# A two-layer trunk's mixer: the convolution branch joined before the recurrent one, its norm taken into the last scan

## The chip, the cores and the metric

The kernel runs on one core of one Trainium2 chip. The time is that of one execution on the device in microseconds (us). All data are float32; one launch computes the whole function.

## The reference, cut to what matters

Two layers, each a half-step feed-forward, a mixer and a second half-step feed-forward, with a layer norm after each. 16 learned tokens stand ahead of 512, so there are 528 positions of width 1024. The change lies in the mixer's end.

```python
def _conv_branch(glu_a, glu_b, conv_w, conv_b, ln_g, ln_b, wo):
    u = glu_a * jax.nn.sigmoid(glu_b)
    kern = conv_w[:, None, :].astype(u.dtype)
    u = lax.conv_general_dilated(u, kern, window_strides=(1,),
                                 padding=[(CONV_WIDTH - 1, 0)],
                                 dimension_numbers=("NWC", "WIO", "NWC"),
                                 feature_group_count=D_CONV) + conv_b
    u = jax.nn.silu(_layer_norm(u, ln_g, ln_b))
    return u @ wo

def _rwkv_branch(zr, time_mix, w0, w_up, a0, a_up, g_up, k_k, k_a, r_k, lnx_g, lnx_b, wo):
    ...
    y = _rwkv7_scan(rh, decay.reshape(B, L, H, N), kh, vh, kk, ah)
    mu = jnp.mean(y, axis=-1, keepdims=True)
    var = jnp.mean(jnp.square(y - mu), axis=-1, keepdims=True)
    y = ((y - mu) * lax.rsqrt(var + GN_EPS)).reshape(B, L, D_RWKV)
    y = y * lnx_g.astype(jnp.float32) + lnx_b.astype(jnp.float32)
    ...
    y = (y + bonus.reshape(B, L, D_RWKV)).astype(zr.dtype) * g
    return y @ wo

def _mixer(x, w_in, time_mix, conv_w, conv_b, conv_ln_g, conv_ln_b, conv_wo,
           w0, w_up, a0, a_up, g_up, k_k, k_a, r_k, lnx_g, lnx_b, rwkv_wo, w_out):
    z = x @ w_in
    ...
    h = jax.nn.sigmoid(gate_c) * yc + jax.nn.sigmoid(gate_r) * yr
    return h @ w_out
```

## The kernel before, in words

Activations lie channel-major: 128 channels on the partitions, 8 tiles of them, positions along the free axis (528 in layer 0; 512 in layer 1's tail, where the learned tokens are dropped). Each large product is done in three float32r products: a weight and an input are both split into a rounded high part and a rest (`w_hi`, `w_lo`; `xh`, `xl`), and hi*hi, hi*lo and lo*hi are summed. One output tile of 128 channels ("a column") therefore takes 8 x 3 x 2 = 48 products, two halves of 264 (or 256) positions. A weight column comes by a 512 KB load to `w_raw` (two buffers), ScalarE rounds it (`w_hi`), and VectorE subtracts (`w_lo`, L160); for the gate columns the rest is made by an adding DMA on POOL's queue.

In a mixer, after the projections, the recurrence is done in four scans (quarters q = 0 to 3 of the heads), each of 8 steps. A step is a chain: TensorE products (L1416), ScalarE copy `w` (L1418), TensorE (L1429, L1432), ScalarE copy `va` (L1435), TensorE (L1438), VectorE state update `sv` (L1444, L1445), and the next step's L1416. TensorE's waits in this chain are filled by `filler`: the projections of the gates (`gate`, L246 products, result `glus` stored to DRAM). VectorE does the taps of the convolution (`taps`, L1089) in its gaps. After a scan, `post` normalizes the scan's output by heads (`group_norm`), transposes it on TensorE (L1540) and stores it to DRAM (`yscr`).

The order on each engine comes from the Tile framework's scheduler, which takes instructions by priority in program order; `high_priority(offset=...)` shifts a part, and `nosync` fixes one instruction behind another without a semaphore. An engine runs its instructions strictly in that order.

At the end of the fourth scan stand 30 products of a constant block of ones (`keep`, L227), then the transposes of the second half, the last gate projection, 22 more constant products. Then `mixer_end` opens a new set of rooms: the recurrent branch is loaded, split (`rh`, `rl`, L113) and multiplied by `rwkv_wo`, first two columns together. The convolution's output (`cscr`) is loaded there too, summed over tiles (`ssum`, L469), and normed by `layer_norm` (L415 mean, L420 subtract, L422 square, L439 variance, L443 square root, L444 reciprocal, L450 scale, L457 SiLU, L112/L113 split into `bh`, `bl`) while TensorE works on the remaining columns. Then come eight columns with `conv_wo`, eight with `w_out`, and the norm `ln2`.

PSUM rooms: `mm` has two buffers in the mixer and six in `mixer_end`.

## Time and profile before

| | |
|---|---|
| median of 3 runs | 3038.53 us (3034.16 to 3048.38) |
| the profiled execution | 3036.81 us, its span 3035.1 us |
| mean granted TensorE clock | 0.992 |
| VectorE, ScalarE busy | 75%, 47% of the span |
| chain that ended last | TensorE 81%, VectorE 8%, DMA 4%, ScalarE 3% |
| mixer's end, layer 0 | last scan ends near 982 us, `conv_wo` columns end near 1104 us |
| mixer's end, layer 1 | last scan ends near 2487 us |

The page gives busy time by engine, the groups of instructions, and the chain that ended last. With TensorE busy nearly all the time, what a change is worth shows in two places: products that need not be done, and the few gaps of TensorE, each with the instruction that ended it. "Busy" of TensorE adds overlapping products only once, so the pace of products is read from a stretch of time and its count. A window's row gives the stretch's length, then for each engine its busy time and count, the granted clock (1.00 is full speed), and the DMA share.

### The profile page before, as it was taken

How to read it: one execution, taken by the hardware profiler on the slowest of the kernel's cores; microseconds unless marked ns; L12 is line 12 of the kernel's file. 1: busy time of each engine (PE TensorE's matmuls, PEld its weight loads, DVE VectorE, ACT ScalarE, POOL GpSimd, SP SyncE). 2: the span in 40 equal slices, each digit the busy share in tenths (PEclk: the TensorE clock that was granted, in tenths of full speed). 3: DMA queues.
4: the chain of work that ended last, by engine and by line, in shares of the span. 5: the costliest groups of instructions: out<-in, count | busy, mean ns of one | idle time of the engine just before them, and what ended most of it. 6: DMA issues, size and time to landing. Idle time of an engine off the chain costs nothing.

```text
span 3035.1 us, 65020 instructions
## 1 busy us (share of the span) xinstructions
PE 2961.4 (98%) x26524; PEld 2832.8 (93%) x26524; DVE 2282.9 (75%) x4689; ACT 1435.9 (47%) x2553; POOL 181.5 (6%) x288
## 2 busy tenths in 40 slices
PE   9999999999999999999999999999999999999998
PEld 9999989888888999999999999899888889999998
DVE  6666777898876768676776767779988758677767
ACT  4544454344554535444444444543454556255443
POOL 0110000000000000100001000000000010001100
PEclk9999999999999999999999999999999999999999
DMA  7565534335465554565555654443354555456661
GB/s 200 141 146 128 128 128 146 97 97 126 109 152 132 181 157 117 129 153 126 129 130 137 146 133 121 134 143 99 98 136 116 137 148 174 138 134 148 149 147 53
DMA packets 556152, 405.33 MB, mean 134 GB/s; under 512 B 89306, under 2 KB 500798, under 8 KB 555854
## 3 DMA queue, kind: packets, MB, share of 16 engines
q1 hardware_dynamic: 520302, 308.49, 35.6%
q0 software_dynamic: 30944, 84.18, 15.0%
q10 hardware_dynamic: 4608, 8.52, 0.8%
q8 instruction: 208, 3.41, 0.5%
q14 instruction: 90, 0.74, 0.1%
HBM read 270.81 MB, written 47.12 MB: 105 GB/s over the span
## 4 chain that ended last, share of the span: by engine, by line
PE 81%; DVE 8%; DMA 4%; ACT 3%; issue 2%; SPq 1%; ACTq 0%; POOL 0%; POOLq 0%; DVEq 0%
PE mm L217 54%; PE mm L246 15%; PE sc L1341 2%; DVE cacc L1089 1%; PE sc L1260 1%; PE tr L1416 1%; PE ch L1429 1%; PE ch L1438 1%; DMA w_raw<-in_w_in_dram 1%; DMA a<-ascr 1%; DMA w_lo<-w_raw 1%; DVE w_lo L160 1%; PE sc L1012 1%; DVE ln_rstd L444 1%; SPq L1309 1%
## 5 line engine op out<-in xcount | busy, mean ns | idle before, releaser
L217 PE MATMUL mm<-xh,w_hi 128*128 128x264 f32 (+1 forms) x1792 | 510.4, 286 | 6.9 <-ACT xh L460 5.4
L217 PE MATMUL mm<-xl,w_hi 128*128 128x264 f32 (+1 forms) x1792 | 509.2, 285 | 0.7 <-DVE xl L461 0.3
L217 PE MATMUL mm<-xh,w_lo 128*128 128x264 f32 (+1 forms) x1792 | 507.8, 284 | 0.0
L217 PE MATMUL mm<-hh,w_hi 128*128 128x264 f32 (+1 forms) x1408 | 399.9, 284 | 1.3 <-ACT hh L112 1.3
L217 PE MATMUL mm<-hh,w_lo 128*128 128x264 f32 (+1 forms) x1408 | 400.0, 284 | 0.0
L217 PE MATMUL mm<-hl,w_hi 128*128 128x264 f32 (+1 forms) x1408 | 399.6, 284 | 0.2
L246 PE MATMUL mm<-xh,w_lo 128*128 128x264 f32 x1760 | 380.9, 294 | 10.9 <-DMA w_lo<-w_raw 10.6
L246 PE MATMUL mm<-xh,w_hi 128*128 128x264 f32 x1760 | 383.5, 294 | 4.1 <-DVE tmp L962 2.3
L246 PE MATMUL mm<-xl,w_hi 128*128 128x264 f32 x1760 | 380.2, 292 | 0.0
L1089 DVE SCALAR_TENSOR_TENSOR cacc<-cu,cw,cacc 128x528 f32<-128x528 f32 (+1 forms) x480 | 355.5, 752 | 5.1 <-ACT cacc L1087 1.4
L217 PEld LDWEIGHTS mm<-xh,w_hi 128*128 128x128 f32 x1792 | 337.2, 189 | 10.8 <-ACT xh L460 7.9
L217 PEld LDWEIGHTS mm<-xl,w_hi 128*128 128x128 f32 x1792 | 339.1, 189 | 2.7 <-DVE xl L461 2.5
L217 PEld LDWEIGHTS mm<-xh,w_lo 128*128 128x128 f32 x1792 | 338.8, 189 | 0.0
L122 ACT CAST w_hi<-sums 128x512 fp32r<-128x512 f32 (+1 forms) x204 | 154.7, 759 | 314.8 <-PE mm L217 205.4
L246 PEld LDWEIGHTS mm<-xh,w_lo 128*128 128x128 f32 x1760 | 277.4, 190 | 19.5 <-DMA w_lo<-w_raw 12.0
L246 PEld LDWEIGHTS mm<-xh,w_hi 128*128 128x128 f32 x1760 | 278.2, 190 | 14.5 <-DVE tmp L962 2.8
L246 PEld LDWEIGHTS mm<-xl,w_hi 128*128 128x128 f32 x1760 | 277.7, 189 | 5.6
L217 PEld LDWEIGHTS mm<-hh,w_hi 128*128 128x128 f32 x1408 | 264.9, 188 | 1.9 <-ACT hh L112 1.7
L217 PEld LDWEIGHTS mm<-hl,w_hi 128*128 128x128 f32 x1408 | 265.1, 188 | 0.9 <-DVE hl L113 0.8
L217 PEld LDWEIGHTS mm<-hh,w_lo 128*128 128x128 f32 x1408 | 265.5, 189 | 0.1
L160 DVE TENSOR_TENSOR w_lo<-w_raw,w_hi 128x1024 fp32r<-128x1024 f32 (+1 forms) x194 | 204.1, 1054 | 67.3 <-ACT w_hi L149 64.2
L149 ACT CAST w_hi<-w_raw 128x1024 fp32r<-128x1024 f32 x134 | 140.4, 1049 | 232.5 <-PE mm L246 63.6
(367 smaller groups left out, 6752.8 us busy)
## 6 DMA issues: line engine op xcount, KB each, us to landing
w_raw<-in_w_in_dram SPq DMA_DIRECT2D x116, 512.0 KB
w_lo<-w_raw POOLq DMA_DIRECT2D x100, 512.0 KB, 5.0
w_raw<-in_ffn_wg_dram SPq DMA_DIRECT2D x88, 512.0 KB
w_raw<-in_ffn_wu_dram SPq DMA_DIRECT2D x88, 512.0 KB
w_raw<-in_ffn_wd_dram SPq DMA_DIRECT2D x80, 512.0 KB
w_lo<-w_raw POOLq DMA_DIRECT2D x68, 256.0 KB, 3.5
w_raw<-in_rwkv_wo_dram SPq DMA_DIRECT2D x16, 512.0 KB
w_raw<-in_conv_wo_dram SPq DMA_DIRECT2D x16, 512.0 KB
```

Of the source, the lines that this page charges most:

```text
L122: self.nc.scalar.copy(hi, x)
L149: copy = self.nc.scalar.copy(hi[:, :kt], raw[:, :kt])
L160: sub = self.nc.vector.tensor_tensor(lo[:, k], raw[:, k], hi[:, k].bitcast(F32), op=ALU.subtract)
L217: self.issued = self.nc.tensor.matmul(pm, a[:, k, :], b[:, xk + k, s], start=first and k == 0 and j == 0, stop=last and k == nk - 1 and j ...
L246: m = self.issued = nc.tensor.matmul(pm[:, h, :n], a[:, wk + k, :], b[:, xk + k, s:s + n], start=first and k == 0 and j == 0, stop=last an ...
L444: nc.vector.reciprocal(rstd[:, :n], rstd[:, :n])
L1012: nc.tensor.matmul(pm, w[a][r, o, :], x[b][r, s], start=j == 0, stop=j == 2)
L1089: tap = nc.vector.scalar_tensor_tensor(y, x, w, y, op0=ALU.mult, op1=ALU.add)
L1260: pairs.append(nc.tensor.matmul(ps[:, e, p * P:(p + 1) * P], FB[p][r, fs], G[r, p, 1, :, cs], start=True, stop=True))
L1309: nc.sync.dma_start(out=dd[o:o + NM, g * N // 2:(g + 1) * N // 2, f, r], in_=self.xd[q, g, f, k:k + N // 2] .rearrange("s t i -> t s i"))
L1341: nc.tensor.matmul(ps[r, i], vt[r, i], x[r, i], start=True, stop=True)
L1416: nc.tensor.matmul(tr[0:C, right(h)], G[:, h // 2, h % 2, 0, cs], sv[:, h, :], start=True, stop=True)
```

## The change

The convolution branch is finished first. All its taps are done by the start of the fourth scan; its output is summed and averaged there (`conv_mean`) and normed during that scan (`conv_norm`), in rooms that are given back at its first step (pool `early`, on the right side of the memory, followed by pool `late`). Both products with a constant block at this place are gone, with their numbers (`KEEPM`). Behind the scan the eight `conv_wo` columns come first, in the mixer's own PSUM rooms (`conv_out`), the first two together; the recurrent branch is loaded and multiplied in `mixer_end` behind them and added. The gates' order is turned to match, one more gate projection is placed ahead of the fourth scan (`FILLS`), and `post` of the fourth scan uses the same rooms as the others. In `layer_norm` the tiny square root that fetches ScalarE's table is fixed behind the last subtraction, so that it no longer stands far ahead of its use.

```diff
-YR = (0, 3, 6)
+YR = (0, 3, 6, 8)
-FILLS = (3, 3, 4, 2)
+FILLS = (3, 3, 5, 2)
+SUMS_EARLY = 1000
-TAP = ((6, 6, 6, 6, 6, 6, 6, 6), (4, 4, 4, 4, 4, 4, 4, 4), (4, 4, 4, 4, 4, 4, 4, 4), (6, 6, 6, 6, 6, 0, 0, 0))
+TAP = ((6, 6, 6, 6, 6, 6, 6, 6), (4, 4, 4, 4, 4, 4, 4, 4), (4, 4, 4, 4, 4, 4, 4, 4), ())
-KEEPM = (30, 22)
...
+                    if q == 3:
+                        self.tap_late = 150
+                        self.taps(KT * TAPS)
+                        mean = self.conv_mean()
                     self.inverse(q, 1, Q)
...
+                if q == 3 and c == 0:
+                    self.leave(epool)
+                    lpool, self.lp3 = self.enter(f"late{l}", side="right")
+                    hc, yc = self.conv_rooms()
+                elif q < 3:
+                    self.taps(TAP[q][c])
...
+        filler(len(fill))
+        room = self.mp.tile([P, 4, KT, P], F32R, name="sb", bufs=1)
+        early = [self.unit("conv_wo", o, [room[:, 2 * o], room[:, 2 * o + 1]])
+                 for o in range(JHEAD)]
+        self.conv_norm(*mean, hc, yc)
         for _ in post:
             pass
-        filler(len(fill) - LAST)
-        self.later = self.turned
-        filler(len(fill))
-        self.later = None
-        self.keep(self.sc()[:, 0], KEEPM[1])
-        self.taps(KT * TAPS)
         self.cuts = 1
-        self.leave(cpool)
+        self.conv_out(early, hc, yc)
...
+    def conv_mean(self):
+        ...
+        for a, b in zip(CV, CV[1:]):
+            nc.sync.dma_start(out=cv[:, a:b], in_=csv[:, a:b, s])
+        ssum, mean = (mp.tile([P, T], F32, name="v", bufs=4)[:, 0:2 * n] for _ in range(2))
+        for o in range(1, KT):
+            nc.vector.tensor_tensor(ssum, cv[:, 0] if o == 1 else ssum, cv[:, o], op=ALU.add)
+        nc.scalar.copy(mean.rearrange("p (h t) -> p h t", h=2), self.over_partitions(ssum))
+
+    def conv_norm(self, cv, rstd, mean, hc, yc):
+        ...
+        for k in range(0, KT, 2):
+            nc.vector.tensor_tensor(cv[:, k:k + 2], cv[:, k:k + 2],
+                                    mean[:, None].to_broadcast([P, 2, 2 * n]), op=ALU.subtract)
+            nc.scalar.activation(hc[:, k:k + 2, s], cv[:, k:k + 2], AF.Square)
+            if k:
+                nc.vector.tensor_tensor(hc[:, 0:2, s], hc[:, 0:2, s], hc[:, k:k + 2, s],
+                                        op=ALU.add)
+        total = hc[:, 0, s]
+        nc.vector.tensor_tensor(total, total, hc[:, 1, s], op=ALU.add)
+        with self.tc.high_priority(offset=SUMS_EARLY):
+            var = self.over_partitions(total)
+        nc.scalar.activation(rstd.rearrange("p (h t) -> p h t", h=2), var, AF.Sqrt,
+                             bias=self.eps[:, 0:1])
+        nc.vector.reciprocal(rstd, rstd)
+        for o in range(KT):
+            z = cv[:, o]
+            nc.vector.scalar_tensor_tensor(z, z, self.v1("conv_ln_g", o, self.vec), rstd,
+                                           op0=ALU.mult, op1=ALU.mult)
+            nc.scalar.activation(z, z, AF.Silu, bias=self.v1("conv_ln_b", o, self.vec))
+            self.split(z, yc[0][:, o, s], yc[1][:, o, s])
+
+    def conv_out(self, early, h, x):
+        ...
+        self.later = self.scanned
+        for os in [range(JHEAD)] + [(o,) for o in range(JHEAD, KT)]:
+            cols = [(o, early[o] if o < JHEAD else self.unit("conv_wo", o), self.gate_load(o), self.mm()) for o in os]
+            self.together([self.mac1(pm[:, i, :n], w, x, t, KT)
+                           for o, w, g, pm in cols for i, t in enumerate(tok)])
+            for o, w, g, pm in cols:
+                for i, t in enumerate(tok):
+                    self.nc.vector.scalar_tensor_tensor(
+                        h[:, o, t], g[:, t], 1.0, pm[:, i, :n], op0=ALU.add, op1=ALU.mult)
...
             elif p == 0 and g:
                 self.group_norm(ysb[:, 2:4], P, 2)
-                self.issued = self.scanned
-                self.keep(self.sc()[:, 0], KEEPM[0])
...
-            nc.scalar.activation(rstd[:, 0:1], eps, AF.Sqrt)
+            self.nosync(nc.scalar.activation(rstd[:, 0:1], eps, AF.Sqrt), sub)
```

On TensorE at the end of layer 0's fourth scan, before (L1438 is the last step's output product, L227 the constant products, L1540 the transposes of the scan's second half, L246 gate projections):

```order
L1438 MATMUL ch<-va,sb 64x64 x4
L227 MATMUL sc<-ones 128x512 x30
L1540 MATMUL tr<-ident,b_11530 128x128 x2
L1540 MATMUL ch<-ident,b_11530 128x128 x2
L246 MATMUL mm<-xl,w_hi 128x264
L246 MATMUL mm<-xh,w_lo 128x264 x2
```

The same place of the change, around the variance's sum (L933), the last step (L1503, L1516 and so on; L251 are gate projections):

```order
L1525 MATMUL ch<-va,sb 64x64 x8
L251 MATMUL mm<-xl,w_hi 128x264
L933 MATMUL sc<-a,ones 128x264 x2
L251 MATMUL mm<-xh,w_lo 128x264 x2
L251 MATMUL mm<-xh,w_hi 128x264 x2
L1503 MATMUL tr<-sv,G 64x64 x4
```

and its start of the convolution's columns (L1615 and L1618 are the transposes of the scan's first half, L219 the products of `conv_out`):

```order
L251 MATMUL mm<-xh,w_lo 128x264 x2
L1615 MATMUL tr<-ident,small 128x16
L1618 MATMUL tr<-ident,b_11591 128x128 x2
L1615 MATMUL ch<-ident,small 128x16
L1618 MATMUL ch<-ident,b_11591 128x128 x2
L219 MATMUL mm<-bh,sb 128x264 x2
```

What moved: the constant products are gone, the transposes of the second half follow only 24 products into the third `conv_wo` column, and the columns themselves stand where the last gate projection and the recurrent columns stood. In layer 1 one whole gate projection still stands between the scan's end and these columns, behind a first single product of `bh`.

On ScalarE, from the copy ahead of the variance to the first part of the normed tile (L964 is the square root, L1505 and L1522 the copies `w` and `va` of the last step, L1188 a gate's tanh, L154 the rounding of the first two `conv_wo` columns, L971 the SiLU, L122 the copy to `bh`):

```order
L964 ACT_TABLE_LOAD
L964 ACTIVATE v<-sc,eps 128x528
L1505 COPY w_12242<-tr 64x256
L1188 ACT_TABLE_LOAD
L1188 ACTIVATE glus<-mm 128x528
L1522 COPY va<-ch 64x256
L1190 DMA gscr_4672<-glus 128x528
L1538 COPY b_11591<-ch 64x256
L154 CAST sb<-w_raw 128x512 x4
L971 ACT_TABLE_LOAD
L971 ACTIVATE G<-G,vec 128x528
L122 CAST bh<-G 128x528
```

Three table loads now stand within the last step and behind it, where before no load stood.

On VectorE, behind the last part of the normed tile (L123), ahead of the first results of the convolution's columns (L994); L1578, L1580 and L1581 belong to the group norm of the scan's second half, L165 makes the `w_lo` of the third and fourth column:

```order
L123 TENSOR_TENSOR bl<-G,bh 128x528
L1623 TENSOR_TENSOR yf<-yf,gg 128x272
L1578 TENSOR_TENSOR b_11591<-b_11591,gn_st 128x512
L165 TENSOR_TENSOR w_lo<-w_raw,w_hi 128x1024
L1580 TENSOR_REDUCE gn_st<-b_12528 128x8
L165 TENSOR_TENSOR w_lo<-w_raw,w_hi 128x1024
L1581 TENSOR_SCALAR gn_st<-gn_st 128x8
L994 SCALAR_TENSOR_TENSOR a<-ln_sq,mm 128x264
L402 TENSOR_SCALAR rs_12535<-gn_st 128x8
L994 SCALAR_TENSOR_TENSOR a<-ln_sq,mm 128x264
```

Before, the group norm had VectorE to itself while the 30 constant products ran; now both the norm's tail and two weight columns stand ahead of it, and the two L994 that empty the first column's PSUM room come behind them.

More of the change, by code (lines that the diff above doesn't have):

```diff
@@ L138, in wunit @@
             load = self.loading = self.nc.sync.dma_start(out=raw[r, :kt], in_=src)
-            if self.behind is not None:
-                self.nosync(load, self.behind)
-                self.behind = None
         n = kt // self.cuts
@@ L149, in wunit @@
             copy = self.nc.scalar.copy(hi[:, :kt], raw[:, :kt])
-            if self.first is not None:
-                self.nosync(copy, self.first[0])
         if dma:
@@ L220, in mac1 @@
                 self.log.append(self.issued)
+                if self.later is not None:
+                    self.nosync(self.issued, self.later)
+                    self.later = None
             yield
@@ L299, in setup @@
         self.cuts = 1
-        self.behind = None
-        self.first = None
         self.issued = None
         self.log = []
+        self.later = None
     def fetch_x(self, h, room, after=None):
@@ L819, in mixer @@
         self.ring(self.w0)
-        mpool, self.mp = self.enter(f"mix{l}")
+        mpool, rest = self.enter(f"mix{l}")
+        epool, room = self.enter(f"early{l}", side="right")
+        self.mp = self.cvp = Rooms(room, rest)
         self.smask = self.mp.tile([P, T], F32, name="smask")
@@ L905, in mixer, with conv_rooms, over_partitions @@
-        self.taps(KT * TAPS)
         self.cuts = 1
-        self.leave(cpool)
+        self.conv_out(early, hc, yc)
         self.leave(mpool)
         self.leave(ppool)
-        return self.mixer_end(more(l + 1))
+        return self.mixer_end(more(l + 1), hc, lpool)
+    def conv_rooms(self):
+        return (self.lp3.tile([P, KT, T], F32, name="a", bufs=1),
+                [self.lp3.tile([P, KT, T], F32R, name="b" + x, bufs=1) for x in "hl"])
+    def over_partitions(self, x):
+        ps, n = self.sc(), self.n
+        for h in range(2):
+            self.nc.tensor.matmul(ps[:, h, :n], self.ones, x[:, h * n:(h + 1) * n],
+                                  start=True, stop=True)
+        return ps[:, :, :n]
@@ L931, in places @@
             tile(name, (NM, NM), 2)
+        self.cut = [tile(f"cu{i}", (TAPS - 1 + T,)) for i in range(2)]
+        tile("cacc", (T,), 2)
     def mm(self):
@@ L1604, in mixer_end @@
         yrv = self.ys.rearrange("(o p) t -> p o t", p=P)
-        def fetch(a, b):
-            load = nc.gpsimd.dma_start(out=h[:, a:b, s], in_=yrv[:, a:b, s])
+        for a, b in zip(YR, YR[1:]):
+            nc.gpsimd.dma_start(out=r[:, a:b, s], in_=yrv[:, a:b, s])
             for o in range(a, b):
-                self.parted = self.split(h[:, o, s], yr[0][:, o, s], yr[1][:, o, s])
-            return load
-        loads = [fetch(a, b) for a, b in zip(YR, YR[1:])]
-        if BEHIND is not None:
-            self.behind = loads[BEHIND]
@@ L1615, in mixer_end @@
-        early = [unit("rwkv_wo", o) for o in range(JHEAD)]
-        for a, b in zip(CV, CV[1:]):
-            if a == CV[YRLATE]:
-                fetch(KT - 2, KT)
-            nc.sync.dma_start(out=cv[:, a:b, s], in_=csv[:, a:b, s])
-        if YRLATE == len(CV) - 1:
-            fetch(KT - 2, KT)
-        for o in range(KT):
-            add = self.add_sum(ssum, cv, o, s)
-            if o == 1:
-                self.nosync(add, self.parted[1])
-        for i in range(2):
-            for _ in self.layer_norm(i, cv, ssum, t0, n, "conv_ln_g", "conv_ln_b", jp, st, yc,
-                                     self.vec, silu=True):
-                pass
@@ L1637, in mixer_end @@
                 op0=ALU.mult, op1=ALU.add)
-        gated(KT, "conv_wo", yc, h, False)
-        hp = parts("r")
+        for o in range(KT):
+            w, g = self.unit("rwkv_wo", o), self.gate_load(KT + o)
+            for i in tok:
+                po, gv = mm()[:, :n], g[:, i]
+                self.together([self.mac1(po, w, yr, i, KT)])
+                nc.vector.scalar_tensor_tensor(gv, gv, 1.0, po, op0=ALU.add, op1=ALU.mult)
+                nc.vector.tensor_tensor(h[:, o, i], h[:, o, i], gv, op=ALU.add)
+        hp = parts(late, "b")
         for o in range(KT):
```

127 lines of the change are left out of this document (56 added, 71 removed).

## The prediction

> **What bounds the kernel now.** First the page's busy times by engine, then the waits of TensorE by releaser (us of idle time, number, longest), then TensorE's timeline at both mixers' ends (start, us, engine, line, and in brackets the idle time before the row with its releaser).
>
> ```profile
> PE 2961.4 (98%) x26524; PEld 2832.8 (93%) x26524; DVE 2282.9 (75%) x4689; ACT 1435.9 (47%) x2553; POOL 181.5 (6%) x288
> PE mm L246 <- DMA w_lo<-w_raw: 10.6, 7, 2.6
> ...
> PE st L415 <- DVE ssum L469: 11.9, 6, 4.6
> ```
>
> TensorE is 98% busy, so time goes only where its products go or where one of its few gaps closes. The waits for `ssum` lie, the two longest of them, at the two mixers' ends, and so do the constant products:
>
> ```profile
> 981.95 7.10 PE L227 MATMUL sc<-ones 128*128 128x512 f32 x30
> 988.88 0.38 PE L1540 MATMUL tr<-ident,b 128*128 128x128 f32 x2
> ...
> 997.01 5.20 PE L227 MATMUL sc<-ones 128*128 128x512 f32 x22
> 1002.04 0.53 PE L217 MATMUL mm<-rh,w_hi 128*128 128x264 f32 x3
> ...
> 1017.71 0.92 PE L415 MATMUL st<-ssum,ones 128*128 128x264 f32 x2 [4.64 <-DVE ssum L469]
> ...
> 2486.73 7.14 PE L227 MATMUL sc<-ones 128*128 128x512 f32 x30
> 2493.70 0.38 PE L1540 MATMUL tr<-ident,b 128*128 128x128 f32 x2
> ...
> 2502.19 5.17 PE L227 MATMUL sc<-ones 128*128 128x512 f32 x22
> 2507.20 0.52 PE L217 MATMUL mm<-rh,w_hi 128*128 128x256 f32 x3
> ...
> 2521.82 1.22 PE L415 MATMUL st<-ssum,ones 128*128 128x256 f32 x2 [3.91 <-DVE ssum L469]
> ```
>
> The products behind the waits are slow (two take 0.92 and 1.22 us, where three of that width take 0.53 at 1002.04), so the windows there count too: length, then for each engine (TensorE, its weight load, VectorE, ScalarE, GpSimd) busy time and count, then granted clock, DMA share and its GB/s.
>
> ```profile
> 1018.00:1021.00 3.00, 3.00 (x14) 2.87 (x14) 2.79 (x4) 1.69 (x3) 0.00 (x0) 0.51 0.30 97
> 1021.00:1024.00 3.00, 3.00 (x25) 3.00 (x24) 2.47 (x7) 1.77 (x2) 0.00 (x0) 0.92 0.05 9
> 2521.00:2524.00 3.00, 2.18 (x8) 2.00 (x9) 2.41 (x5) 1.04 (x1) 0.00 (x0) 0.50 0.55 152
> 2524.00:2527.00 3.00, 3.00 (x17) 3.00 (x17) 2.58 (x5) 2.86 (x3) 0.00 (x0) 0.54 0.15 55
> 1060.00:1080.00 20.00, 20.00 (x167) 20.00 (x166) 16.57 (x30) 10.34 (x15) 0.00 (x0) 1.00 0.61 172
> ```
>
> After each wait the granted clock is about a half for 3 to 6 us. The last row is a stretch without gaps: 20/167 = 0.12 us a product, 5.8 us for a column of 48.
>
> **What goes.** Between the first constant product and the next row lie 988.88 − 981.95 = 6.93 and 1002.04 − 997.01 = 5.03 us in layer 0, 6.97 and 5.01 in layer 1: **23.9 us**. The two waits are 4.64 + 3.91 = **8.55 us**. Clock: busy time times what is missing to 1.00 is (1 − 0.51)·3.00 + (1 − 0.92)·3.00 = 1.7 and (1 − 0.50)·2.18 + (1 − 0.54)·3.00 = 2.5, **4.2 us**. Together 36.7. Real work only changes places: gate projections, `rwkv_wo` and `conv_wo` columns and the sums over partitions are as many as before.
>
> **What comes instead.** The constant products gave cover. Behind the first block the group norm of the scan's second half ran on VectorE:
>
> ```profile
> 982.45 0.69 DVE L1476 TENSOR_REDUCE gn_st<-b 128x8 f32<-128x512 f32 x1 [3.91 <-ACT b L1451]
> ...
> 987.97 0.69 DVE L1497 TENSOR_TENSOR b<-b,rs 128x512 f32<-128x512 f32 x1
> ```
>
> that is 6.2 us with a dozen tiny steps between. Now its cover must be `conv_wo` products, and these need the convolution's norm, whose variance leaves TensorE only in the last scan step. The prices of the norm's steps (groups by line: busy us, mean ns of one, idle before):
>
> ```profile
> L160 DVE TENSOR_TENSOR w_lo<-w_raw,w_hi 128x1024 fp32r<-128x1024 f32 x15 | 18.3, 1220 | 9.6 <-ACT w_hi L149 9.6
> L147 ACT CAST w_hi<-w_raw 128x512 fp32r<-128x512 f32 x14 | 8.5, 616 | 3.6 <-PE mm L246 3.6
> L1591 DVE SCALAR_TENSOR_TENSOR h<-g,mm 128x264 f32<-128x264 f32 x16 | 6.6, 420 | 1.0 <-PE mm L217 0.8
> L1101 ACT ACTIVATE glus<-mm 128x528 f32<-128x528 f32 x9 | 5.5, 607 | 6.7 <-PE mm L246 6.7
> L113 DVE TENSOR_TENSOR rl<-h,rh 128x528 fp32r<-128x528 f32 x8 | 5.2, 704 | 2.6 <-ACT rh L112 2.5
> L420 DVE TENSOR_TENSOR a<-a,st 128x1056 f32<-128x1056 f32 x4 | 4.9, 1236 | 0.2 <-PE st L415 0.2
> L112 ACT CAST rh<-h 128x528 fp32r<-128x528 f32 x8 | 4.6, 630 | 1.3 <-DMA h<-yscr 1.3
> L444 DVE RECIPROCAL ln_rstd<-ln_rstd 128x264 f32<-128x264 f32 x2 | 3.6, 1800 | 0.1
> L1089 DVE SCALAR_TENSOR_TENSOR cacc<-cu,cw,cacc 128x528 f32<-128x528 f32 (+1 forms) x480 | 355.5, 752 | 5.1 <-ACT cacc L1087 1.4
> ```
>
> The new orders hold table loads, whose row of before is:
>
> ```profile
> 1032.35 1.28 ACT L457 ACT_TABLE_LOAD   x1
> 1033.65 0.92 ACT L457 ACTIVATE a<-a,vec 128x264 f32<-128x264 f32 x2
> ```
>
> I follow the chain by hand from V, the end of the variance's sum (L933), in layer 0.
> - VectorE: load 1.28 and square root (as long as two of 264, some 1.0, and hand-overs) end at V + 2.6; a reciprocal of 528 (two of 1.80) at 6.2; the scaling (0.75, as L1089) at 6.95.
> - ScalarE: copy `w` at 3.0, second load at 4.3, tanh 0.6, copy `va` at 5.3, then four casts for the `conv_wo` columns (0.62 each, free to write only after the last step reads its rooms, about V + 6.3) to 9.2, third load to 10.5, SiLU 0.65, copy 0.6: `bh` at V + 11.8. The difference (0.7, as L113) gives `bl` at 12.5.
> - TensorE: last output product at about V + 5.5, 23 gate products (2.8), transposes and hand-overs: at the columns by about V + 10.4.
> - Then each of the other seven tiles costs VectorE 0.75 + 0.70 = 1.46 (ScalarE 1.25), with some 1.7 of the group norm's pieces among them: last `bl` at V + 24.4, last 12 products (1.43) at 25.9. TensorE alone would be done at 10.4 + 11.5 = 21.9: **4.0 us** of waiting.
> - The third column needs the first one's PSUM room. Ahead of the two L994 that empty it stand L1623, three pieces of the group norm (0.4 + 0.7 + 0.7 + 0.2), two L165 of 1.22 and one more tiny step; with 0.42 for each L994 that is 5.4, so V + 29.8: **3.9 us**.
> - After 24 products the transposes wait for the rest of the group norm, a dozen steps of 0.2 and 0.69: **0.7 us**.
>
> Layer 0: 8.6. In layer 1 the order differs: one `bh` product, then a whole gate projection (5.8 us) that covers the norm. The product waits for `bh` (13.3 against 10.3), **3.0**; then `w_lo` 0.3, second PSUM room 1.0, third column's 0.6, transposes 0.2: 5.1. Sum **13.7 us**. Behind the waiting products stand on TensorE the rest of the first two columns, the group norm's transposes and every later column, so nothing of it is hidden. These are hand estimates; their ends are nothing (the norm done before TensorE comes) and a chain that starts one scan step (5.4 us, D's rows) later in each layer, 13.7 + 10.8 = 24.5. I take the middle because V stands in the last step in both layers' orders.
>
> The clock after new waits goes by the nearest row: a wait of 3.9 like the removed one of 3.91 (2.5 us), a wait of 3.0 like this one (fences: the wait, another of its kind, and two windows):
>
> ```profile
> 916.53 0.30 PE L1334 MATMUL sc<-dd,ut 64*64 64x64 f32 x2 [1.50 <-DMA dd<-xdscr]
> ...
> 2420.89 0.39 PE L1334 MATMUL sc<-dd,ut 64*64 64x64 f32 x2 [2.76 <-DMA dd<-xdscr]
> ```
>
> ```profile
> 2420.00:2425.00 5.00, 4.11 (x39) 3.67 (x40) 0.83 (x2) 0.00 (x0) 0.00 (x0) 0.60 0.20 18
> 2425.00:2430.00 5.00, 5.00 (x48) 4.65 (x48) 2.78 (x4) 0.61 (x1) 0.00 (x0) 0.72 0.73 202
> ```
>
> (1 − 0.60)·4.11 + (1 − 0.72)·5.00 = 3.0. Together **5.5 us**. The Trainium skill, page "TensorE: Matmul & The Clock Gate", section "What's actually happening", sets half rate only after an idle window of about 3.4 us, and full rate after as long of work; by it the 3.0-us wait would be free and the sum some 4 us lower. No run of before bears that out for waits: the clock was 0.60 after 2.76 us, and the row decides.
>
> **Smaller terms.** The convolution's output is now loaded on SP's queue ahead of the fourth scan. Before, that load stood in the chain that ended last (start, us):
>
> ```profile
> 1004.83 5.62 DMA a<-cscr
> ```
>
> The last column's load of this kind, and seven additions of 0.7, are some 11 us, two scan steps; the mean's sum stands in the scan's second step. I take 0; one wait like 2.76 with its clock in each layer, 12, would be the other end. The loads for the recurrent columns move behind the `conv_wo` columns on the same queue, with 46 us of products ahead of them: 0. The two waits for `dd`, above, stand ahead of the third and fourth scans, where the turned gates now put one more projection (5.8 us): I let them go with their clock, 1.5 + 2.8 + 3.0 = −7. Against it, gate projections that follow one another wait for `w_lo` (10.6/7 = 1.5 each by the wait row; I take two, +3), and the fourth scan takes the norm's work between its steps (+2): **−2**, with ends at −7 and at the stretch priced under D. The square root fixed behind the subtraction: its load was hidden beside other work before and stays there, 0, at most one load of 1.28 in each of five norms (+6). Later columns have a 5.8-us product stretch for every weight's 2 × 0.62 and 1.22, so 0.
>
> **Sum.** −36.7 + 13.7 + 5.5 − 2 = −19.5. The profiled execution took 3036.8 us (span 3035.1), 1.7 below the median of the three. 3036.8 − 19.5 = 3017.3; I forecast **3017**.
>
> **Rivals.**
> - **B: the norm's waits are hidden.** If V comes earlier than the last step, or the gate projections reach over it as in layer 1, only the removal counts: 3036.8 − 36.7 = 3000. For: layer 1's order has that cover. Against: in layer 0 the first `conv_wo` product stands directly behind the scan's end.
> - **C: the waits are as long as those removed.** The order puts three loads, a reciprocal, 16 VectorE operations and the group norm behind V; one step's delay in each layer gives back 10.8 and some 4 of clock, so about 3032 (3027 to 3037). This is also the case in which the change does not do what it says, the norm running behind the scan and not in it.
> - **D: slower.** The state update that starts the next step queues on VectorE behind the norm's 128x1056 operations.
>
> ```profile
> 966.35 0.43 DVE L1444 TENSOR_TENSOR sv<-ch,sv 64x256 f32<-64x256 f32 x1
> ...
> 971.72 0.43 DVE L1444 TENSOR_TENSOR sv<-ch,sv 64x256 f32<-64x256 f32 x1
> 960.00:982.00 22.00, 21.80 (x252) 18.78 (x252) 11.94 (x47) 15.04 (x35) 2.89 (x4) 1.00 0.61 158
> ```
>
> A step takes 5.4 us. Two operations of 1.24 stand ahead of the update at most, 2.5 a step, 7 steps, two layers: 35 us; and if TensorE's clock falls as behind the 2.76-us wait, 14 × 2 more, so up to 3017 + 63 = 3080, at half of both 3048. Without clock it decides from 19.5/14 = 1.4 us a step. For: the scan is a chain through this update. Against: VectorE is busy 11.94 of 22 us there, the old load (taps) leaves the scan, and gate projections stand between the steps' products.
> - **F: switching tables costs more than the load.** Three loads a layer with as much again behind each: 3 × 1.28 × 2 = 7.7, so 3025. Against: the row above, the next activation starts 0.02 us after the load's end (1032.35 + 1.28 = 1033.63, next 1033.65). The Trainium skill, page "ScalarE: Activation LUTs", section "What ACT_TABLE_LOAD costs", puts a drain of about 1.38 us beside the 1.28 of the load; the load agrees, the drain does not show.
>
> **How the numbers follow.** Forecast (3008 to 3027) 0.48; B (2994 to 3006) 0.16; C (3027 to 3037) 0.22; D 0.09; F (3021 to 3029) 0.05. Half a per cent, about what a measurement of this kernel can tell from no change, is 15.2 us: 3023.3 and 3053.7 from the median. Faster: 0.40 of the forecast and all of B, 0.56. Slower by over that is the dear half of D, 0.05. The rest, 0.39, is the same. The range from 2998 to 3039 leaves out some 0.05 of B, 0.04 of C and 0.09 of D.
>
> **What would show it.** Right: no L227 at this place; two gaps of TensorE in layer 0, at the first `bh` products and at the third column's first product, near 4 us each, one of 3 in layer 1, with clock near 0.5 to 0.7 behind them; scan steps of 5.4 us. B: no gap over 1 us there. C: gaps of 8 us or more, or the variance's sum after the last step. D: steps of 7 us, idle time before L1503 released by the state update. F: over 1 us between a table load's end and the next activation. The forecast fails if the fourth scan itself becomes longer, which no row of before can show.

## The result, and the profile after

| | before | changed |
|---|---|---|
| median | 3038.53 us (3034.16 to 3049.03) | 3023.68 us (3011.41 to 3026.83, 7 runs) |
| ratio to before | | 0.9938 (95% interval 0.9916 to 0.9960) |
| profiled execution, span | 3036.81, 3035.1 us | 3019.63, 3017.9 us |

The change is faster by 0.6%, some 15 us by the medians and 17.2 by the two profiled executions, where 19.5 were forecast. TensorE's waits by releaser in the changed kernel (us of idle time, number, longest), and two of the kernel before that the prediction does not show:

```profile
PE mm L251 <- DMA w_lo<-w_raw: 16.8, 10, 2.8
...
PE tr L1503 <- DVE sv L1532: 6.9, 12, 1.7
...
PE sc L1421 <- DMA dd<-xdscr: 0.5, 1, 0.5
```

```profile
PE tr L1416 <- DVE sv L1445: 7.7, 14, 1.7
...
PE sc L1334 <- DMA dd<-xdscr: 5.1, 4, 2.8
```

The waits for `ssum` at the mixers' ends are gone, those for `dd` at that line's counterpart (L1421 for L1334) are down from 5.1 to 0.5 us, those for `w_lo` are up from 10.6 to 16.8. To see where time went, each execution is cut at the same rows of TensorE's timeline: the first sums of the first layer norm, and for each mixer's end the stretch from the third scan's last step to the next layer norm's first sums. Of the kernel before:

```profile
370.84 0.71 PE L415 MATMUL st<-ssum,ones 128*128 128x264 f32 x2
...
894.15 0.65 PE L1416 MATMUL tr<-sv,G 128*64 128x64 f32 x8 [0.25 <-DVE sv L1445]
...
1140.30 0.69 PE L415 MATMUL st<-ssum,ones 128*128 128x264 f32 x2
...
2398.13 0.65 PE L1416 MATMUL tr<-sv,G 128*64 128x64 f32 x8 [0.25 <-DVE sv L1445]
...
2641.75 0.67 PE L415 MATMUL st<-ssum,ones 128*128 128x256 f32 x2
```

And of the changed one:

```profile
376.45 0.71 PE L419 MATMUL st<-ssum,ones 128*128 128x264 f32 x2
...
896.00 0.65 PE L1503 MATMUL tr<-sv,G 128*64 128x64 f32 x8 [0.25 <-DVE sv L1532]
...
1132.02 0.68 PE L419 MATMUL st<-ssum,ones 128*128 128x264 f32 x2
...
2390.36 0.65 PE L1503 MATMUL tr<-sv,G 128*64 128x64 f32 x8 [0.25 <-DVE sv L1532]
...
2624.30 0.67 PE L419 MATMUL st<-ssum,ones 128*128 128x256 f32 x2
```

The ends take 246.15 and 243.62 us before, 236.02 and 233.94 after: 10.1 and 9.7 us less, 19.8 together. The start takes 5.6 us more. What is left, −3.0, lies for the most part between the first sums and the third scan's last step of layer 0 (523.3 us before, 519.6 after). In the 14 profiles of this document that stretch takes 520.9 to 526.3 us with the old order and 518.1 to 525.8 with the new one, so no effect of the change is shown there. Windows of these stretches (length; busy time and count of TensorE, its weight load, VectorE, ScalarE, GpSimd; clock, DMA share, GB/s), before and after:

```profile
894.15:1140.30 246.15, 236.56 (x2226) 224.05 (x2226) 170.30 (x385) 113.36 (x199) 10.44 (x14) 0.99 0.58 162
2398.13:2641.75 243.62, 234.48 (x2205) 222.27 (x2206) 164.00 (x351) 111.91 (x196) 10.45 (x14) 0.97 0.58 161
```

```profile
896.00:1132.02 236.02, 225.21 (x2173) 213.13 (x2174) 166.28 (x366) 110.19 (x181) 10.39 (x14) 1.00 0.59 162
2390.36:2624.30 233.94, 223.89 (x2153) 212.90 (x2154) 160.55 (x332) 108.20 (x178) 10.35 (x14) 0.96 0.59 162
```

TensorE's busy time falls by 11.4 and 10.6 us, about the constant products (12 a layer). Its idle time does not fall at all: 9.6 and 9.1 us before, 10.8 and 10.1 after. What was removed of waits came back in sum as other waits. These are the new ones at the ends of the scans, in layer 0 and layer 1:

```profile
996.29 0.90 PE L219 MATMUL mm<-bh,sb 128*128 128x264 f32 x2 [0.89 <-ACT bh L122]
999.09 0.51 PE L219 MATMUL mm<-bh,sb 128*128 128x264 f32 x2 [0.58 <-ACT bh L122]
1000.37 0.39 PE L219 MATMUL mm<-bl,sb 128*128 128x264 f32 x1 [0.77 <-DVE bl L123]
1012.03 0.36 PE L219 MATMUL mm<-bh,w_hi 128*128 128x264 f32 x1 [1.49 <-DVE rs L403]
...
2488.43 0.58 PE L219 MATMUL mm<-bh,sb 128*128 128x256 f32 x1 [2.69 <-ACT bh L122]
2489.46 0.81 PE L251 MATMUL mm<-xh,w_lo 128*128 128x264 f32 x2 [0.45 <-DMA w_lo<-w_raw]
2509.04 0.35 PE L219 MATMUL mm<-bh,w_hi 128*128 128x256 f32 x1 [0.33 <-DVE rs L405]
```

They stand where the forecast had them and sum to 7.2 us. Others stand ahead of the fourth scan:

```profile
912.48 0.51 PE L251 MATMUL mm<-xh,w_lo 128*128 128x264 f32 x2 [2.80 <-DMA w_lo<-w_raw]
...
2406.56 0.81 PE L251 MATMUL mm<-xh,w_lo 128*128 128x264 f32 x2 [2.53 <-DMA w_lo<-w_raw]
...
2431.89 0.69 PE L1525 MATMUL ch<-va,sb 128*64 128x64 f32 x16 [1.37 <-ACT va L1522]
2434.12 0.81 PE L251 MATMUL mm<-xh,w_lo 128*128 128x264 f32 x2 [1.54 <-DMA w_lo<-w_raw]
```

At the first two places the kernel before waited 1.58 and 1.20 us:

```profile
909.63 0.51 PE L246 MATMUL mm<-xh,w_lo 128*128 128x264 f32 x2 [1.58 <-DMA w_lo<-w_raw]
...
2413.24 0.51 PE L246 MATMUL mm<-xh,w_lo 128*128 128x264 f32 x2 [1.20 <-DMA w_lo<-w_raw]
```

### The profile page after: what moved, and what is told of

The parts are those of the page before. It is cut to its first block, busy times and chain, and to the rows that moved or that the text cites. A ratio compares the mean times of both kernels' runs of the same rounds, so it can differ in the third digit from the quotient of the medians.

```text
span 3017.9 us, 64740 instructions
## 1 busy us (share of the span) xinstructions
PE 2941.0 (97%) x26420; PEld 2814.6 (93%) x26420; DVE 2275.2 (75%) x4651; ACT 1421.1 (47%) x2513; POOL 181.4 (6%) x288
## 3 DMA queue, kind: packets, MB, share of 16 engines
q0 software_dynamic: 30944, 84.18, 15.1%
## 4 chain that ended last, share of the span: by engine, by line
PE 56%; DVE 5%; ACT 2%; DMA 2%; issue 2%; SPq 0%; ACTq 0%; POOL 0%; DVEq 0%; POOLq 0%
PE mm L219 43%; PE mm L251 8%; DMA w_lo<-w_raw 1%; PE sc L1428 1%; PE sc L1347 1%; PE tr L1503 1%; DVE y L455 1%; PE ch L1516 1%; DVE cacc L1176 1%; DVE ln_rstd L449 1%; DVE w_lo L165 1%; PE ch L1525 0%; DVE xl L466 0%; PE sc L1099 0%; DMA w_raw<-in_w_in_dram 0%
## 5 line engine op out<-in xcount | busy, mean ns | idle before, releaser
L219 PE MATMUL mm<-xh,w_hi 128*128 128x264 f32 (+1 forms) x1792 | 509.3, 286 | 12.6 <-ACT xh L465 8.7
L219 PE MATMUL mm<-xl,w_hi 128*128 128x264 f32 (+1 forms) x1792 | 509.5, 285 | 0.6 <-DVE xl L466 0.3
L219 PE MATMUL mm<-xh,w_lo 128*128 128x264 f32 (+1 forms) x1792 | 508.4, 284 | 0.0
L219 PE MATMUL mm<-hh,w_hi 128*128 128x264 f32 (+1 forms) x1408 | 399.8, 284 | 2.0 <-ACT hh L122 2.0
L219 PE MATMUL mm<-hh,w_lo 128*128 128x264 f32 (+1 forms) x1408 | 399.8, 284 | 0.0
L219 PE MATMUL mm<-hl,w_hi 128*128 128x264 f32 (+1 forms) x1408 | 399.5, 284 | 0.2
L251 PE MATMUL mm<-xh,w_lo 128*128 128x264 f32 x1760 | 382.3, 295 | 17.4 <-DMA w_lo<-w_raw 16.8
L251 PE MATMUL mm<-xh,w_hi 128*128 128x264 f32 x1760 | 383.3, 295 | 4.2 <-DVE tmp L1049 1.9
L251 PE MATMUL mm<-xl,w_hi 128*128 128x264 f32 x1760 | 382.7, 293 | 0.0
L219 PEld LDWEIGHTS mm<-xh,w_hi 128*128 128x128 f32 x1792 | 336.7, 189 | 17.2 <-ACT xh L465 11.7
L219 PEld LDWEIGHTS mm<-xl,w_hi 128*128 128x128 f32 x1792 | 339.3, 189 | 3.2 <-DVE xl L466 2.6
L219 PEld LDWEIGHTS mm<-xh,w_lo 128*128 128x128 f32 x1792 | 339.0, 189 | 0.1
L251 PEld LDWEIGHTS mm<-xh,w_lo 128*128 128x128 f32 x1760 | 279.0, 191 | 26.9 <-DMA w_lo<-w_raw 19.0
L251 PEld LDWEIGHTS mm<-xh,w_hi 128*128 128x128 f32 x1760 | 279.3, 191 | 14.0 <-DVE tmp L1049 2.3
L251 PEld LDWEIGHTS mm<-xl,w_hi 128*128 128x128 f32 x1760 | 279.6, 190 | 6.2
L219 PEld LDWEIGHTS mm<-hh,w_hi 128*128 128x128 f32 x1408 | 264.8, 188 | 2.6 <-ACT hh L122 2.3
L219 PEld LDWEIGHTS mm<-hl,w_hi 128*128 128x128 f32 x1408 | 265.0, 188 | 0.9 <-DVE hl L123 0.7
L219 PEld LDWEIGHTS mm<-hh,w_lo 128*128 128x128 f32 x1408 | 265.5, 189 | 0.1
L165 DVE TENSOR_TENSOR w_lo<-w_raw,w_hi 128x1024 fp32r<-128x1024 f32 (+1 forms) x190 | 199.0, 1051 | 64.3 <-ACT w_hi L156 61.1
```

What stands on the lines that cost most here:

```text
L165: sub = self.nc.vector.tensor_tensor(lo[:, k], raw[:, k], hi[:, k].bitcast(F32), op=ALU.subtract)
L219: self.issued = self.nc.tensor.matmul(pm, a[:, k, :], b[:, xk + k, s], start=first and k == 0 and j == 0, stop=last and k == nk - 1 and j ...
L251: m = self.issued = nc.tensor.matmul(pm[:, h, :n], a[:, wk + k, :], b[:, xk + k, s:s + n], start=first and k == 0 and j == 0, stop=last an ...
```

## The experiments

All are compared with the kernel before on the same chip. The last three columns are the rows above, read from each run's own timeline: the first sums, and the lengths of the two mixers' ends.

| run | ratio to before (95%) | first sums at | layer 0's end | layer 1's end |
|---|---|---|---|---|
| before | | 370.84 | 246.15 | 243.62 |
| the change | 0.9938 (0.9916 to 0.9960) | 376.45 | 236.02 | 233.94 |
| change_again | 0.9945 (0.9930 to 0.9959) | 378.32 | 235.94 | 232.11 |
| b_nokeep | 0.9996 (0.9982 to 1.0010) | 369.62 | 248.36 | 240.78 |
| b_sqrt_fixed | 1.0022 (1.0013 to 1.0032) | 376.97 | 248.43 | 245.05 |
| a_sqrt_free | 0.9941 (0.9919 to 0.9962) | 370.85 | 237.01 | 235.59 |
| a_sqrt_first | 0.9935 (0.9920 to 0.9950) | 373.88 | 238.25 | 233.64 |
| a_gate_back | 0.9929 (0.9907 to 0.9951) | 374.88 | 236.86 | 231.98 |
| a_norm_early | 0.9945 (0.9923 to 0.9967) | 375.49 | 237.95 | 229.09 |
| a_room_first | one run, 3023.33 us, no interval | 377.62 | 239.70 | 230.14 |
| a_conv_load_twice | one run, 3031.76 us, no interval | 376.73 | 245.67 | 233.94 |
| a_cover_back | 0.9984 (0.9973 to 0.9995) | 377.00 | 243.23 | 236.78 |
| a_best | 0.9920 (0.9904 to 0.9937) | 372.61 | 239.19 | 229.35 |
| best_again | 0.9920 (0.9905 to 0.9936) | 371.38 | 237.39 | 229.23 |

The change's two profiles differ by 0.1 and 1.8 us in the ends; a difference of under some 3 us in one profile's end carries nothing by itself. The two runs without an interval stand beside a median of 3042.75 us of the kernel before on their chip.

**b_nokeep: only the products go.**

```diff
 (the kernel before)
-KEEPM = (30, 22)
+KEEPM = (0, 0)
```

> The kernel before with no constant products at the mixers' ends, everything else its own (23.9 us of products less). Theory 'cover': these products hid the group norm (6.2 us on VectorE) and the trip of the scan's output through DRAM; without them TensorE waits about 4 us for the transposes (15 gate products now stand ahead of them) and about 5 to 7 us for the first recurrent columns in each layer, and each wait costs 2 to 3 us of clock behind it: 3033 to 3045 us, no gain. Theory 'pure cost': the products go and nothing takes their place: about 3015 us, no new wait over 1 us.

Deleting 23.9 us of products from the old order gains nothing that can be measured (0.9996, at most 0.2% by the interval), and the ends change by +2.2 and −2.8 us. TensorE's timeline of this run at layer 0's end:

```profile
985.43 0.66 PE L1540 MATMUL tr<-ident,b 128*128 128x128 f32 x2 [5.98 <-DVE b L1497]
...
998.50 1.03 PE L217 MATMUL mm<-rh,w_hi 128*128 128x264 f32 x3 [3.90 <-ACT rh L112]
```

The first two waits, 9.9 us, stand where 12.0 us of constant products stood (layer 1: 5.65 and 3.88), and the clock falls behind them, as a window shows:

```profile
985.00:990.00 5.00, 4.57 (x21) 4.61 (x22) 1.89 (x5) 1.02 (x2) 1.41 (x3) 0.50 0.19 65
```

So theory "cover" holds, and with it the main reading of the change: its gain is not the deletion by itself, but the deletion in an order that has real work at that place.

**a_cover_back: constant products in the new order.**

```diff
-        self.later = self.scanned
+        self.issued = self.scanned
+        self.keep(self.sc()[:, 0], 30)
+        self.later = self.issued
         for os in [range(JHEAD)] + [(o,) for o in range(JHEAD, KT)]:
```

> The change with 30 constant products (6.9 us a layer) put back behind the last scan, ahead of the first conv_wo products. If the chain behind the variance is as the forecast had it (last part of the normed tile at V + 24.4, TensorE through the first pair 4 us too early), 6.9 us of cover hide it: waits for bh and bl go in both layers (2.24 and 2.69 us), the third column's wait falls under 0.5, and layer 0's stage grows by 6.9 - 3.7 = 3 us, layer 1's by 6.9 - 3.5 and less clock lost, 1 to 3 us; the whole 3 to 6 us above the change. If the constant products are pure cost here, the stages grow by 6.9 each, 14 us in all, and the waits stay.

The waits for `bh` and `bl` are gone in both layers, so 6.9 us are enough for the chain behind the variance, as the forecast had it. But the third column still waits in layer 0, and so do the transposes, for the group norm:

```profile
1015.02 0.41 PE L1620 MATMUL tr<-ident,b 128*128 128x128 f32 x2 [1.11 <-DVE b L1586]
1018.10 0.56 PE L219 MATMUL mm<-bh,w_hi 128*128 128x264 f32 x1 [1.59 <-ACT y L1662]
```

The profile puts the third column's wait down to an operation of ScalarE in `mixer_end`, whose result this product does not read. What the column needs is its PSUM room, as in the forecast, and in VectorE's timeline of this run the second of the operations that empty it (L996) is the first of this row, behind pieces of the scan's output. That it is the cause fits the times, and was not tested:

```profile
1017.53 0.76 DVE L996 SCALAR_TENSOR_TENSOR a<-ln_sq,mm 128x264 f32<-128x264 f32 x2
```

The ends are 7.2 and 2.8 us longer than the change's (7.3 and 4.7 by its second profile), and the whole 12 to 14 us by the ratios, more than expected and between the two theories. By the ratios the constant products cost nearly their own length (13.8 us) in this order, by the ends 10 to 12; in the old order they cost nothing that can be measured. These are 30 of the 52 of a layer; the new order with all of them was not run.

**a_norm_early: the variance earlier.**

```diff
-        for k in range(0, KT, 2):
...
-        nc.vector.tensor_tensor(total, total, hc[:, 1, s], op=ALU.add)
+        with self.tc.high_priority(offset=1000):
+            for k in range(0, KT, 2):
...
+            nc.vector.tensor_tensor(total, total, hc[:, 1, s], op=ALU.add)
```

> The change with the convolution norm's subtractions, squares and sums at a higher priority, so that the variance's sum stands four scan steps earlier in both layers. Theory 'chain behind the variance': the waits for bh and bl (2.24 us in layer 0, 2.69 in layer 1) go, with the clock lost behind the second: 5 to 9 us less, 3015 to 3019, and TensorE's waits for the state update (6.9 us in sum) rise by under 2 us. Rival D: the 128x1056 operations now stand ahead of the state updates, a step takes over 1 us more, those waits rise by 5 us or more, no gain.

In layer 1 the wait of 2.69 us is gone and the end 3 to 5 us shorter than the change's (229.09 against 233.94 and 232.11). In layer 0 a wait of 1.40 us for `bh` is left (up to 1006.63), and rival D shows in one step, with 1.92 us for the state update:

```profile
983.01 0.65 PE L1504 MATMUL tr<-sv,G 128*64 128x64 f32 x8 [1.92 <-DVE sv L1533]
```

In layer 0 the variance is no longer what holds `bh`: its sum now ends at 977.8, some 12 us (two steps) earlier than in the change, counted from the third scan's last step, not four steps earlier. But ScalarE comes to the square root only at 990.24, behind the scan's copies, and to the first copy `bh`, at 1005.96, behind the four casts for the `conv_wo` columns:

```profile
990.24 0.70 ACT L965 ACTIVATE v<-sc,eps 128x528 f32<-128x528 f32 x1
...
1003.38 2.18 ACT L154 CAST sb<-w_raw 128x512 fp32r<-128x512 f32 x4
```

TensorE's waits for `sv` rise from 6.9 to 8.7 us in sum, as expected under 2 us; those for `w_lo` rise to 20.6, but a_room_first, whose norm stands where the change has it, has the longest of them too (4.24 us there, 4.10 here). So in layer 1 the wait hangs on the variance, in layer 0 of this run on ScalarE's order. The whole is not below the change.

**a_gate_back: the gate projection.**

```diff
-FILLS = (3, 3, 5, 2)
+FILLS = (3, 3, 4, 2)
```

> The change with four gate projections ahead of the fourth scan as before, so one more stands in or behind it. Theory of the forecast: the extra projection ahead took away the waits for dd (1.5 and 2.8 us) and added waits for w_lo; put back, waits for dd of 1 to 3 us return, waits for w_lo fall by 2 to 4 us in sum from 16.8, and the waits for bh and bl in layer 0 (2.2 us) are covered by 5.8 us of gate products: 3020 to 3028. Rival: the gate's place does not matter, the waits for dd were removed by the changed order of the loads; then dd stays at 1.6 us in sum.

A miss: the waits for `dd` do not return, and layer 0's waits for `bh` and `bl` stay as they were (2.24 us). The windows ahead of the first product with `dd`, of gate products alone (length, busy time and count, clock, DMA share, GB/s), of before, the change, and this run:

```profile
894.15:916.53 22.38, 15.17 (x112) 1.00 0.76 187
```

```profile
896.00:921.23 25.23, 18.28 (x136) 1.00 0.81 211
```

```profile
892.93:918.20 25.27, 18.10 (x136) 1.00 0.81 211
```

24 more products, half a projection, stand there in the change, and also with the number put back: the scheduler takes them as they come ready, and this number does not decide it. That the 24 products cover the old wait of 1.50 us fits, but it is not shown by a run that removes them; what brought them there stays open. The forecast's "one more projection ahead" was half as much. In layer 1 the number does move something: the gate projection that the change has behind the first `bh` product ends ahead of it in this run, the wait for `bh` is 6.14 us instead of 2.69, and the end is still no longer (231.98 us). The clock offsets it: ahead of this wait the change has windows at 0.66 and 0.50, 3.7 us lost as worked out below, and this run none under 1.00.

**b_sqrt_fixed, a_sqrt_free, a_sqrt_first: the tiny square root.** In the kernel before, and in the change:

```diff
 (b_sqrt_fixed)
-            nc.scalar.activation(rstd[:, 0:1], eps, AF.Sqrt)
+            self.nosync(nc.scalar.activation(rstd[:, 0:1], eps, AF.Sqrt), sub)
 (a_sqrt_free)
-            self.nosync(nc.scalar.activation(rstd[:, 0:1], eps, AF.Sqrt), sub)
+            nc.scalar.activation(rstd[:, 0:1], eps, AF.Sqrt)
 (a_sqrt_first)
-            self.nosync(nc.scalar.activation(rstd[:, 0:1], eps, AF.Sqrt), sub)
+            tiny = nc.scalar.activation(rstd[:, 0:1], eps, AF.Sqrt)
+            self.norms += 1
+            if self.norms > 2:
+                self.nosync(tiny, sub)
```

> The kernel before with the tiny square root of layer_norm fixed behind the last subtraction, nothing else of the change. TensorE's order in the first feed-forward is then that of the change. Theory 'order': the first layer norm's sums come at 375 to 378 us instead of 370 to 374, with a wait of 2 us at 61 us, and the whole is 3 to 6 us above the kernel before (ratio 1.001 to 1.002). Theory 'chance': they come at 370 to 374, ratio 1.000.

> The change with the tiny square root of layer_norm not fixed behind the subtraction (as before). The first 365 us of the changed kernel took 5.6 us more than before, with a wait of 1.98 us at 61 us that before lacks. Theory 'order': the fixed square root moved ScalarE's first instructions and with them the order of the first feed-forward; undone, that wait goes and the place lies at 360 instead of 365 us, the whole near 3019. Theory 'run to run': the wait or the 5 us come again or are of the clock; nothing to tell from the changed kernel (3024).

> The change with the tiny square root left free in the first layer norm of the program only (its two halves), fixed in all others. If the 5.5 us at the start come from that first one alone, the first layer norm's sums stand at 371 us as in the kernel before (376 in the change), the mixers' ends stay as in the change (236 and 234 us, waits for bh of 2.2 and 2.7 us), and the whole is about 5 us below the change: 3015 to 3020. If they come from another norm, the first sums stand at 376 again.

Fixed in the old kernel, it alone costs 0.22% (0.13 to 0.32), some 7 us. A row of its start:

```profile
61.23 0.39 PE L217 MATMUL mm<-xh,w_hi 128*128 128x264 f32 x1 [2.07 <-DVE ln_sq L520]
```

In the eight profiles with it fixed from the first norm on, the first sums come at 374.9 to 378.3 us (mean 376.7); in the six others at 369.6 to 373.9 (mean 371.5). The ranges do not overlap: 5 us for this edit, in the first feed-forward, 300 us ahead of the first norm. In the program before, this square root was the first instruction of ScalarE; fixed behind a subtraction it leaves, and the scheduler puts the first feed-forward's products in another order. TensorE's waits up to the first sums are 5.9 to 8.1 us with it fixed (mean 7.3) and 3.6 to 6.3 in the others (mean 4.4), so 2.9 of the 5 us are waits; the rest, longer busy time, was not traced to a cause. a_sqrt_first came latest of the six (373.9 us, between its two forecasts), with a wait of 2.21 us at the same place, so the wait itself also varies. With the square root freed everywhere, other waits stand in the mixers' ends (4.67 us for `bh` in layer 1, 2.18 for the convolution's sum), and the whole was not measurably below the change.

**a_conv_load_twice: the moved load.**

```diff
         for a, b in zip(CV, CV[1:]):
-            nc.sync.dma_start(out=cv[:, a:b], in_=csv[:, a:b, s])
+            for _ in range(2):
+                nc.sync.dma_start(out=cv[:, a:b], in_=csv[:, a:b, s])
```

> The change with each of the loads of the convolution's output ahead of the fourth scan done twice (the same data to the same place, 2.1 MB more on SP's queue in each layer). If these loads take bandwidth from the adding DMA that makes w_lo, the wait for w_lo at the start of the gate projections ahead of the fourth scan rises from 2.80 and 2.53 us to 4 us or more in both layers. If they don't meet, it stays within 0.5 us, and only the mean's sum comes later (a wait of 2 to 8 us for the convolution's sum in the scan).

```profile
916.16 0.81 PE L251 MATMUL mm<-xh,w_lo 128*128 128x264 f32 x2 [5.63 <-DMA w_lo<-w_raw]
...
2422.55 0.81 PE L251 MATMUL mm<-xh,w_lo 128*128 128x264 f32 x2 [6.16 <-DMA w_lo<-w_raw]
```

TensorE's timeline of this run: the waits double. In the other ten profiles with the new order they are 2.21 to 4.24 us in layer 0 and 1.32 to 2.83 in layer 1; in the three with the old order and load 1.18 to 1.58 and 1.07 to 1.30. So the load of the convolution's output and the adding DMA meet, but the change's 2.53 us in layer 1 lie near the long end. A run without the load at that place was not tried.

**a_room_first: the third column's wait.**

```diff
-            for o, w, g, pm in cols:
-                for i, t in enumerate(tok):
-                    self.nc.vector.scalar_tensor_tensor(
-                        h[:, o, t], g[:, t], 1.0, pm[:, i, :n], op0=ALU.add, op1=ALU.mult)
+            with self.tc.high_priority(offset=400 if len(os) > 1 else 0):
+                for o, w, g, pm in cols:
+                    for i, t in enumerate(tok):
+                        self.nc.vector.scalar_tensor_tensor(
+                            h[:, o, t], g[:, t], 1.0, pm[:, i, :n], op0=ALU.add, op1=ALU.mult)
```

> The change with the four operations that empty the first two columns' PSUM rooms (L994) at a higher priority, so that they stand together ahead of the weights' rest (L165) and the group norm's pieces on VectorE. If the third column waits for the room behind these, as the forecast had it, its wait (1.49 us in layer 0, 0.33 in layer 1) falls under 0.4 us and the transposes of the scan's second half wait under 1 us instead. If something else holds it, a wait over 1 us stays at its first product.

Inconclusive, since the edit moved less than it was meant to. VectorE's timeline of this run:

```profile
1017.82 1.45 DVE L995 SCALAR_TENSOR_TENSOR a<-ln_sq,mm 128x264 f32<-128x264 f32 x4
```

The four operations stand together now, but both weights' rests (L165, 1.22 and 1.21 us) stay ahead of them, and the wait is 1.33 us instead of 1.49. TensorE was through the first pair at about 1017.4, VectorE with the second rest at 1017.8.

**a_best and best_again: three edits together,** those of a_sqrt_first and a_room_first, and that of a_norm_early in layer 1 alone (`offset=1000 if self.l else 0`); beside the second, the change itself.

> The change with three edits together: the first norm's square root free, the first two columns' rooms emptied first, and in layer 1 alone the convolution norm's statistics at a higher priority (there it took the wait for bh away and made the stage 4.9 us shorter). If the gains add up: 5.5 at the start, 1 to 1.5 in layer 0's end, 4 to 5 in layer 1's, 10 to 12 us below the change, so 3010 to 3014 and about 0.991 of the kernel before. Rival: the scheduler gives it back elsewhere, as it did where the square root was free everywhere; then 3018 to 3024.

> The version with three edits (first norm's square root free, first two columns' rooms first, in layer 1 the norm's statistics early) beside the change on one chip. If it is better than the change, the first sums come some 4 us and layer 1's stage 3 to 5 us earlier, and the medians differ by 6 to 10 us (0.2 to 0.3 per cent). If the edits are given back, the medians are within 3 us.

> The change itself once more, on the same chip as the version with three edits, so that the two can be compared: 0.9938 of the kernel before, with an interval of about 0.2 per cent; the stages from the third scan's last step to the next layer norm's first sums at 236 to 240 and 230 to 234 us.

0.9920 twice, against 0.9938 and 0.9945. The first median, 3017.37 us, lies between its two forecasts (3010 to 3014 if the gains add up, 3018 to 3024 if they are given back), the second inside its own. On the chip that ran both, medians of 3016.21 and 3023.14 us. The first sums come 7 us earlier there, layer 1's end is 2.9 us shorter and layer 0's 1.5 us longer. The intervals overlap (0.9905 to 0.9936 and 0.9930 to 0.9959), so the version is better than the change by the medians, but that is not settled; it is clearly below the kernel before.

## Why the prediction was right, point by point

The total was right (3017 forecast, 3019.6 profiled, median 3023.7, within the forecast's own 3008 to 3027), and so was the cause: cover of another kind in place of constant products. Several sizes were off, and that the sum still came within 3 us of the profiled execution is partly luck: the new waits were some 5 us too dear in it, the start and the waits for `w_lo` some 8 too cheap.

- **What goes.** 23.9 us of products: TensorE's busy time in the two ends fell by 22.0. Waits for `ssum`, 8.55: gone. That the products gave cover, b_nokeep shows.
- **The chain from V.** In layer 0 V is about 985.0 (the variance's sum), and the timelines of ScalarE and then VectorE in the changed kernel answer to the steps:

```profile
984.93 1.28 ACT L964 ACT_TABLE_LOAD   x1
986.23 0.70 ACT L964 ACTIVATE v<-sc,eps 128x528 f32<-128x528 f32 x1
...
995.61 0.63 ACT L122 CAST bh<-G 128x528 fp32r<-128x528 f32 x1
```

```profile
986.96 3.45 DVE L966 RECIPROCAL v<-v 128x528 f32<-128x528 f32 x1 [1.53 <-ACT v L964]
...
1006.42 0.70 DVE L123 TENSOR_TENSOR bl<-G,bh 128x528 fp32r<-128x528 f32 x1
```

  TensorE reaches the columns behind the transposes of the first row below, and is through the first pair with the second row:

```profile
994.97 0.44 PE L1618 MATMUL ch<-ident,b 128*128 128x128 f32 x2
...
1010.25 0.29 PE L219 MATMUL mm<-bh,sb 128*128 128x264 f32 x1
```

  TensorE at the columns at V + 10.4 (forecast 10.4), `bh` at V + 11.2 (11.8), last `bl` at V + 22.1 (24.4), the pair through at V + 25.5 (25.9), the third column at V + 27.0 (29.8). The pair took 15.1 us for 11.5 of products, so 3.6 us were lost of the 4.0 forecast, 2.24 of them as idle rows, the rest as products that stood a little longer. At the third column it was 1.49 (3.9), for the transposes none (0.7). In layer 1: 2.69 (3.0; the forecast's 13.3 against 10.3, for which it shows no working, came as 12.8 against 10.2), then 0.45, 0 and 0.33 for 0.3, 1.0 and 0.6, and none for the transposes. Idle rows of 7.2, or 8.6 with the pair's slow products, in place of 13.7: the mechanism holds, the term was mis-sized, most at the third column, where VectorE came through the seven tiles, the group norm's pieces and the weights' rests sooner than summed and TensorE later than alone.
- **Table loads.** What rival F turns on, seen again: 984.93 + 1.28 = 986.21, and the next activation starts at 986.23. The Trainium skill, page "ScalarE: Activation LUTs", section "What ACT_TABLE_LOAD costs", has the load right; of its drain nothing shows here either.
- **`dd` and `w_lo`.** The waits for `dd` at the two places went, as taken (−4.3). The waits for `w_lo` grew by 6.2 instead of 3. Two of them are those of 1.58 and 1.20, now 2.80 and 2.53. The forecast counted consecutive projections and not the load of the convolution's output, moved beside the adding DMA, which a_conv_load_twice shows to lengthen these waits.
- **The clock.** 7.2 us of lost clock were to go and 5.5 to come. Windows of the changed kernel in layer 1:

```profile
2405.00:2410.00 5.00, 3.44 (x17) 3.44 (x18) 4.75 (x10) 2.11 (x3) 0.84 (x1) 0.66 0.47 110
2435.00:2440.00 5.00, 5.00 (x32) 3.82 (x33) 0.40 (x2) 0.95 (x2) 0.00 (x0) 0.50 1.07 202
2485.00:2490.00 5.00, 1.87 (x10) 1.33 (x9) 4.52 (x8) 4.89 (x8) 0.26 (x1) 0.81 0.85 154
2490.00:2495.00 5.00, 5.00 (x25) 5.00 (x24) 3.26 (x7) 3.02 (x7) 0.00 (x0) 0.50 0.82 216
```

  0.34·3.44 + 0.50·5 + 0.19·1.87 + 0.50·5 = 6.5 us in layer 1, none in layer 0 behind the new waits (1.00 in the windows of 5 us there): hardly anything won. The wait of 2.69 us cost 2.9 here, as the row of 2.76 had said (3.0). The waits for `w_lo` and `va` cost the rest, and their clock was not priced. In the forecast's own terms a free wait of 3.0 us would have lowered its sum by that wait's 3.0 us of clock, not by the 4 that it gives.
- **The step that failed:** "The square root fixed behind the subtraction: its load was hidden beside other work before and stays there, 0". It costs 5 us at the start, not by its load but with another order of the first feed-forward's products; the forecast looked for it beside the norms, where the table is used. Its upper end (+6) was nearer: 5 us at the start, some 7 in the whole where the edit stands alone.
- **The rivals.** B: not so, though in a_norm_early and the version with three edits layer 1's wait for `bh` is gone. C: not so. D: not in the change, whose waits for `sv` fell from 7.7 to 6.9 us; it shows once the norm is put earlier. F: not so.

With the sizes as measured: −22.0 busy and +2.1 idle make −19.8 in the ends, +5.6 at the start, −3.0 elsewhere, together −17.2. The forecast's −19.5 held 0 for the start and had no term for the last.
